# Layer 1's gate and up products of a two-layer encoder by seven block products instead of eight

## The chip, the cores and the metric

One core of one Trainium2 chip. The metric is the device time of one execution in microseconds (us): the time before is the median of three runs, 2474.93 us (2474.85 to 2480.22). Engines are named as in the profile: PE (TensorE, matmuls; PEld is its weight load), DVE (VectorE), ACT (ScalarE), POOL (GpSimd), SP (SyncE, which here only issues DMAs). All times below come from one profiled execution of the kernel before.

## The reference

A trunk of two residual layers on x of shape (1, 1024, 1024) in float32. Layer 0 mixes with a gated MLP and pooled means, layer 1 with RWKV-7 time mixing (a recurrence over chunks of 64 tokens), and each layer is followed by a SwiGLU block; the hidden width is 2816, that is 22 blocks of 128.

```python
D_MODEL = 1024; SEQ = 1024; CHUNK = 64; FFN_HIDDEN = 2816

def swiglu(hn, w_gate, w_up, w_down):
    return (jax.nn.silu(hn @ w_gate) * (hn @ w_up)) @ w_down
...
def wkv7_scan(r, w, k, v, a, b):          # RWKV: one state of 64x64 per head
    def step(state, inp):
        r_t, w_t, k_t, v_t, a_t, b_t = inp
        sa = jnp.einsum('bhvk,bhk->bhv', state, a_t)
        state = (state * w_t[:, :, None, :] + sa[..., None] * b_t[:, :, None, :]
                 + v_t[..., None] * k_t[:, :, None, :])
        return state, jnp.einsum('bhvk,bhk->bhv', state, r_t)
...
# layer: h = h + mixer(rms_norm(h)); h = h + swiglu(rms_norm(h)); at the end rms_norm(h)
```

## The kernel before

The 1024 tokens are two halves of 512, A (h = 0) and B (h = 1). Activations lie with features on the partitions: `H[h]` is 8 tiles of 128x512. Every fp32 product is three matmuls of split operands (`mm3`, L343 to L346): hi·hi, lo·hi and hi·lo, each with a 128x128 weight tile and a 128x512 operand. A gate or up block (128 hidden features, all 1024 inputs) for one half is thus 24 matmuls, and so is a down block for one half. In the names of the profile `ahi`/`alo` are the activations, `whi`/`wlo` and `wdhi`/`wdlo` the weights, `hidhi`/`hidlo` the hidden values.

**Weights.** One list, `plan` (`push`, L103), holds every 128x1024 weight block in order of use. `take` (L131) hands out the next one, starts the loads of the two behind it and splits the next: the load goes to a ring of three `raw` buffers on ACT's DMA queue (L113), the hi part is copied out by ACT (L143), the lo part is subtracted by DVE (L144). Each gate and up block of layer 1 is loaded and split twice, once for each half.

**FFN.** `ffn` (L648) runs groups of blocks: gate and up of each block in the group, `silu(gate)·up` (ACT L662, DVE L670), its split (ACT L673, DVE L674), then the group's down products, which DVE adds to the residual (`h<-h,mm`, L424). In layer 1 and half A, blocks 0 and 1 run beside the projections of the second RWKV half, blocks 2 to 17 in groups of three beside the recurrence, 18 and 19 after it, then `out_proj(1)` and the RMS norm of half B, then 20 and 21 with the final norm of half A. Half B runs all 22 blocks after that.

**Recurrence.** `recur` (L1152) takes 512 tokens in 8 chunks of 64: small matmuls (`sm`, `yp`, L1176) between tiles that ACT, DVE and POOL make. Behind every second chunk stands a step `post`: it takes mean and variance of `yp` (DVE L1353 to L1364, with one operation of POOL, L349), scales it (16 ACT operations, L1370), multiplies and adds on DVE and POOL (L1375, L1376), and transposes the result `ysb` on PE into `sm`. `drive` (L732) interleaves the steps of `ffn` and of `recur` by their costs at `RATIO` 3.0. The instruction scheduler of the language decides the order on each engine from there, with a priority that lets dense work run behind the recurrence's (`AHEAD`, 450); each engine then executes its own list strictly in that order, and only semaphores tie the engines to each other. Within the recurrence, PE's small matmuls keep the order of the program (`ordered`).

**Queues.** Weights and activations `y` come on ACT's queue; SP's queue carries the recurrence's operands, the residual's reload (`reload`, L1472: 2 MB in one DMA) and half of the output.

Of the kernel before, what the change touches and what calls it, by code (L numbers as in the profile page):

```python
# [16 lines left out]
P = 128  # L17
# [15 lines left out]
BESIDE = (4, 2)  # L33
# [3 lines left out]
def tile_trunk(  # L37
# [63 lines left out]
    acts, dests, splits = set(), {}, {}  # L101
# [17 lines left out]
    def split_at(i):  # L119
        if i >= len(plan) or i in ready:  # L120
            return
        load_at(i)
        if i not in raws:
            return
        key, _, view, dest = plan[i]
        raw = raws[i]
        hi, lo = (dest or whl)()
        splits.get(key[0], lambda i, *t: split(*t))(key[1], view(raw), view(hi), view(lo))
        ready[i] = hi, lo
# [131 lines left out]
    n0, n1, a, b = groups_of(BESIDE[0])  # L261
    G0B = n0, n1 + [a], [b]
    n0, n1, a, b = groups_of(BESIDE[1])
    G1A = n0, n1, [a], [b]
# [32 lines left out]
    push_beside(1, push_o(0) + push_f(1, 0, G1A[0]))  # L297
    push_proj(1, ("n1", n_d[1]))
    push_ffn(1, 0, G1A[1])
    push_ffn(1, 0, G1A[2], push_act(("y", 1), y_d[1]))  # L300
    for e in push_o(1):
        e()
    push_ffn(1, 0, G1A[3])
    push_ffn(1, 1)
# [24 lines left out]
    def mmt():  # L329
        return pst("mm")  # L330
# [3 lines left out]

    DENSE = {"mm": ("mm", 5), "aux": ("aux", 3)}
# [15 lines left out]
    def norm_sums(h):  # L351
# [7 lines left out]
        return acc  # L359

# [284 lines left out]
    l0_es.close()  # L645

# [780 lines left out]
    def final_down(h, fs, wd, hid, turned):  # L1427

        with tc.manual_schedule(engines={mybir.EngineType.PE}):
# [14 lines left out]
            products(1, 0)  # L1444
            for j in range(4):
# [119 lines left out]
    def blocks():  # L1565
        yield from out_proj(0, ys, sums_a)
        yield from ffn(1, 0, hnA, f, G1A[0], nd=2, after=spill_a)

# [3 lines left out]
    beside(1, blocks(), [1] * 8 + weights_of(G1A[0]), parts, (8, norm_a))  # L1572
# [10 lines left out]
    hp, hp_es = open_pool(name="ha2", bufs=1, side="left")  # L1583
# [3 lines left out]
    drive(ffn(1, 0, hnA, f, G1A[1]), with_reload(hp, 0, h_d[0, 1], recur(1, wp)), RATIO)  # L1587
# [8 lines left out]
    reload(hb_pool, 1, h_d[1, 1])  # L1596
    ys = open_act(("y", 1), b)
    drive(ffn(1, 0, hnA, f, G1A[2], between=take_act(("y", 1))))
# [4 lines left out]
    for e in (fin_es, hb_es, b_es, hp_es, nxt["a_es"], f_es, ps_es):  # L1603
        e.close()
# [30 lines left out]
```

## Time and profile before

| what | before |
|---|---|
| median of three runs | 2474.93 us (2474.85 to 2480.22) |
| the profiled execution | 2477.63 us; span in the trace 2475.9 us |
| mean granted TensorE clock | 0.989 of full speed |
| second v projection ends, recurrence of half B begins | at about 1613 us |
| recurrence ends (last `post` transposed) | 1881 us |
| `out_proj(1)`, norm of half B | until about 1980 us |
| half B's 22 blocks of layer 1 | about 2000 to 2476 us |

The span is what the trace covers; the execution's own time is 1.7 us longer. A row of the trace's timeline gives start, duration, engine, line, operation, tiles and shapes, and in brackets the idle time before it and what ended it. Matmuls are pipelined: a duration of 0.39 us in a row doesn't mean that the next one starts 0.39 us later; the distance of two starts is the price of one. Windows give, for a stretch, each engine's busy time, the granted clock (1.00 is full speed), the share of the 16 DMA engines' time in use and the GB/s moved.

### The profile page before, as it was taken

What the parts mean: (1) busy time and instruction counts of PE and PEld (TensorE: products, weight loads), DVE (VectorE), ACT (ScalarE), POOL (GpSimd) and SP (SyncE); (2) the same over time, 40 slices, a digit from 0 to 9 for tenths busy, and PEclk for the clock granted to TensorE, in tenths of its full rate; (3) what the DMA queues carried; (4) which work ended last, traced back from release to release, by engine and by line L of the source; (5) the groups of instructions that cost most, each with busy time, mean ns of one, the idle gap of its engine ahead of it and who ended that gap; (6) DMA issues with size and microseconds to landing.
All of it is one profiled execution on the core that took longest, in us unless ns stands there. A gap on an engine that the chain in (4) does not pass through costs nothing.

```text
span 2475.9 us, 37980 instructions
## 1 busy us (share of the span) xinstructions
PE 2406.4 (97%) x15735; PEld 1977.5 (80%) x15735; DVE 1382.7 (56%) x2126; ACT 912.1 (37%) x1369; POOL 244.6 (10%) x262
## 2 busy tenths in 40 slices
PE   8999999999999998999999999989999999999998
PEld 7888888888878787888878777778878778888887
DVE  6445634444875874655548847856555446444443
ACT  6233422222664432432325754433232324322223
POOL 0200000000014400211000133201111000000001
PEclk9999999999999999999999999999999999999999
DMA  5123433323355577542434465695444322433231
GB/s 179 49 60 89 150 102 102 119 86 94 109 176 139 140 208 202 156 127 70 135 112 143 153 168 134 191 234 140 119 128 128 111 85 75 147 102 118 87 98 56
DMA packets 436396, 310.69 MB, mean 125 GB/s; under 512 B 93376, under 2 KB 395584, under 8 KB 435456
## 3 DMA queue, kind: packets, MB, share of 16 engines
q10 hardware_dynamic: 297280, 210.53, 28.6%
q1 hardware_dynamic: 138944, 97.75, 13.8%
q8 instruction: 123, 2.02, 0.3%
q14 instruction: 49, 0.40, 0.1%
HBM read 254.68 MB, written 53.54 MB: 124 GB/s over the span
## 4 chain that ended last, share of the span: by engine, by line
PE 82%; DMA 6%; DVE 5%; ACT 2%; issue 2%; POOL 2%; SPq 0%; ACTq 0%; POOLq 0%; DVEq 0%
PE mm L344 22%; PE mm L345 22%; PE mm L346 22%; PE sm L1176 5%; DMA raw<-y_d 1%; DVE wlo L144 1%; PE yp L1176 1%; DMA raw<-in_ffn_w_down_dram 1%; DMA lnw<-in_rwkv_ln_w_dram 1%; ACT whi L143 1%; PE aux L1097 1%; PE mm L511 1%; PE mm L512 1%; PE mm L513 1%; PE aux L1098 1%
## 5 line engine op out<-in xcount | busy, mean ns | idle before, releaser
L345 PE MATMUL mm<-alo,whi 128*128 128x512 f32 x1952 | 766.7, 393 | 0.9 <-issue 0.8
L346 PE MATMUL mm<-ahi,wlo 128*128 128x512 f32 x1952 | 765.4, 392 | 1.7 <-DVE wlo L144 1.7
L344 PE MATMUL mm<-ahi,whi 128*128 128x512 f32 x1952 | 765.8, 393 | 0.8 <-ACT whi L143 0.8
L143 ACT ACTIVATE whi<-raw 128x1024 fp32r<-128x1024 f32 x288 | 304.6, 1059 | 744.7 <-PE mm L345 605.3
L144 DVE TENSOR_TENSOR wlo<-raw,whi 128x1024 fp32r<-128x1024 f32 x288 | 359.1, 1248 | 289.5 <-ACT whi L143 270.1
L346 PEld LDWEIGHTS mm<-ahi,wlo 128*128 128x128 f32 x1952 | 367.7, 188 | 82.5 <-issue 3.5
L345 PEld LDWEIGHTS mm<-alo,whi 128*128 128x128 f32 x1952 | 367.7, 188 | 79.9 <-issue 2.9
L344 PEld LDWEIGHTS mm<-ahi,whi 128*128 128x128 f32 x1952 | 367.7, 188 | 79.0 <-issue 2.1
L344 PE MATMUL mm<-hidhi,wdhi 128*128 128x512 f32 x624 | 240.5, 395 | 8.1 <-DVE h L424 3.8
L345 PE MATMUL mm<-hidlo,wdhi 128*128 128x512 f32 x624 | 245.0, 393 | 0.4 <-DVE hidlo L674 0.4
L346 PE MATMUL mm<-hidhi,wdlo 128*128 128x512 f32 x624 | 244.9, 392 | 0.0
L424 DVE TENSOR_TENSOR h<-h,mm 128x512 f32<-128x512 f32 x192 | 129.3, 686 | 149.7 <-PE mm L346 148.5
L143 ACT ACTIVATE wdhi<-raw 128x1024 fp32r<-128x1024 f32 x82 | 86.4, 1057 | 249.7 <-DMA raw<-in_ffn_w_down_dram 164.4
L144 DVE TENSOR_TENSOR wdlo<-raw,wdhi 128x1024 fp32r<-128x1024 f32 x82 | 100.2, 1223 | 112.1 <-ACT wdhi L143 112.0
L670 DVE TENSOR_TENSOR sg<-sg,mm 128x512 f32<-128x512 f32 x88 | 60.3, 686 | 157.1 <-PE mm L346 155.3
L344 PEld LDWEIGHTS mm<-hidhi,wdhi 128*128 128x128 f32 x624 | 117.5, 189 | 36.8 <-DVE h L424 6.4
L345 PEld LDWEIGHTS mm<-hidlo,wdhi 128*128 128x128 f32 x624 | 117.8, 189 | 25.7 <-DVE hidlo L674 1.3
L346 PEld LDWEIGHTS mm<-hidhi,wdlo 128*128 128x128 f32 x624 | 117.8, 189 | 24.9
L424 DVE TENSOR_TENSOR hA<-hA,mm 128x512 f32<-128x512 f32 x72 | 48.8, 686 | 77.2 <-PE mm L346 77.0
L349 POOL TENSOR_TENSOR nrs<-nrs,small 128x4 f32<-128x4 f32 x8 | 10.0, 1244 | 667.2 <-DVE nrs L371 667.2
L674 DVE TENSOR_TENSOR hidlo<-sg,hidhi 128x512 fp32r<-128x512 f32 x88 | 65.7, 748 | 10.0 <-ACT hidhi L673 10.0
L344 PE MATMUL mm<-xhi,whi 128*128 128x512 f32 (+1 forms) x160 | 65.3, 408 | 0.0
(299 smaller groups left out, 2886.3 us busy)
## 6 DMA issues: line engine op xcount, KB each, us to landing
raw<-in_ffn_w_gate_dram ACTq DMA_DIRECT2D x88, 512.0 KB
raw<-in_ffn_w_up_dram ACTq DMA_DIRECT2D x88, 512.0 KB
raw<-in_ffn_w_down_dram ACTq DMA_DIRECT2D x88, 512.0 KB
raw<-in_ab_w_in_dram ACTq DMA_DIRECT2D x16, 512.0 KB
raw<-in_ab_w_out_dram ACTq DMA_DIRECT2D x16, 512.0 KB
raw<-in_rwkv_w_r_dram ACTq DMA_DIRECT2D x16, 512.0 KB
raw<-in_rwkv_w_k_dram ACTq DMA_DIRECT2D x16, 512.0 KB
ar_d<-ar SPq DMA_DIRECT2D x16, 512.0 KB
```

What stands on the lines that cost most here:

```text
L143: act.activation(hi, src, AF.Copy)
L144: (eng or dve).tensor_tensor(out=lo, in0=src, in1=hi.bitcast(F32), op=ALU.subtract)
L344: pe.matmul(o, whi, xhi, start=first, stop=False)
L345: pe.matmul(o, whi, xlo, start=False, stop=False)
L346: pe.matmul(o, wlo, xhi, start=False, stop=last)
L424: dve.tensor_tensor(out=H[h][:, m, :], in0=H[h][:, m, :], in1=o, op=ALU.add)
L511: pe.matmul(ops[j], xhi[:, k, sl], whi[:, kk], start=(k == 0), stop=False)
L512: pe.matmul(ops[j], xhi[:, k, sl], wlo[:, kk], start=False, stop=False)
L513: pe.matmul(ops[j], xlo[:, k, sl], whi[:, kk], start=False, stop=(k == KT - 1))
L670: dve.tensor_tensor(out=s, in0=s, in1=o, op=ALU.mult)
L674: dve.tensor_tensor(out=lo, in0=s, in1=hi.bitcast(F32), op=ALU.subtract)
L1176: i = f(*args, **kw)
```

## The change

For two blocks f = 2i and 2i+1 of one matrix, the weights are a 2x2 matrix of quarters (two halves of the 1024 inputs, two blocks), the activations another (two halves of the inputs, two halves A and B of the tokens). The changed kernel forms the four products of blocks and token halves with seven quarter products instead of eight (the Winograd form of Strassen's algorithm): a quarter product is 12 matmuls, and a pair of blocks of one matrix takes 84 instead of 96. Sums of weight quarters (s1 to s4) are made on DVE from the loaded blocks, sums of activations (t1 to t4) once, on DVE, by `combine`. For this, halves A and B must both be there, which half B is only after the recurrence and `out_proj(1)`. So:

- **Ahead** (`ahead_steps`): eight even blocks (0, 2 beside the projections, 4, 6, 8, 10 beside the recurrence, 12, 14 after it) are computed for half A alone, down product included. The first of the seven products, which is the first half of such a block's sum, is copied out to DRAM (`p1_d`). Beside the recurrence thus stand 4 blocks instead of 16; the ratio of `drive` goes from 3.0 to 9.3.
- **Front** (`first_steps`): three even blocks (16, 18, 20) the same way, without down, beside `combine`, which makes t1 to t4 as soon as half B's norm is there.
- **Full** (`full_steps`): for all 11 pairs and both matrices, 22 rounds, the five products that are left (60 matmuls), which give the odd block for half A and both blocks for half B. Round by round the two weight blocks are combined on DVE in the buffers they were loaded into, the psum is read at two points while it goes on accumulating (`now`), the kept product comes back from DRAM, and the hidden values are written to DRAM (`hid_d`).
- **Down** (`down_steps`): the 14 blocks of half A that are left, then the 22 of half B, with hidden values read back from DRAM on SP's queue. The final norm of half A comes with the last group of A's.

Count of instructions in the whole program, before and after: matmuls with 512 columns 9120 and 8856; DVE tensor_tensor of 128x1024 384 and 319, of 128x512 746 and 1098; ACT activations of 128x1024 396 and 331, of 128x512 708 and 852; weight blocks loaded 234 and 212; DMAs on SP's queue 444 and 578. Up to the products beside the projections of layer 1 the order on PE is the same.

```diff
-BESIDE = (4, 2)
+PAIRS = 11
+AHEAD_OF = ([0, 2],), ([4, 6], [8, 10]), ([12, 14],), (16, 18, 20)
...
+    def ahead_steps(groups, hn, fp, nd, nh, after=None, between=iter(())):
...
+            if kind == "gu":
+                b11, b21 = (parts_of(hn, slice(k, k + 4)) for k in (0, 4))
+                w, os_ = [take((k, 1, 0, f)) for k in "gu"], [mmt(), mmt()]
+                for n in range(2):
+                    yield from quarter_steps(os_[n], parts_of(w[n], LO), b11, True)
+                    t = fp.tile([P, HT], F32, tag="p1", bufs=2 if nd else 1, name="p1")
+                    act.activation(t, os_[n], AF.Copy)
+                    sp.dma_start(p1_d[:, f + n, :], t)
+                for n in range(2):
+                    yield from quarter_steps(os_[n], parts_of(w[n], HI), b21, False)
...
+    def full_steps(blocks, kept, x, fp, wp):
+        def weights(i):
+            (a11, a12), (a21, a22) = ((raws[j][:, LO], raws[j][:, HI]) for j in (i - 1, i))
+            s3 = wp.tile([P, HT], F32, tag="s3", bufs=1, name="s3")
+            dve.tensor_tensor(out=s3, in0=a11, in1=a21, op=sub)
+            s1, s2, s4 = a21, a11, a12
+            dve.tensor_tensor(out=s1, in0=a21, in1=a22, op=ALU.add)
+            dve.tensor_tensor(out=s2, in0=s1, in1=a11, op=sub)
+            b = whl()
+            split(s2, *parts_of(b, HI))
+            split(s1, *parts_of(b, LO))
...
+            dve.tensor_tensor(out=s4, in0=a12, in1=s2, op=sub)
...
+        for i, n in blocks:
+            k = i in kept
+            a = mmt()
...
+            b, c, d = take(("full1", i, n))
+            quarter(a, parts_of(b, HI), x["t2"], k)
+            if prev:
+                prev[0]()
+            if k:
+                t1 = tile_("t1")
+                sp.dma_start(t1, p1_d[:, 2 * i + n, :])
+            u2, u3 = tile_("t2"), tile_("t3")
+            now(u2)
+            o = mmt()
+            quarter(o, parts_of(b, LO), x["t1"], True)
+            if prev:
+                prev[1]()
+            quarter(a, d, x["t3"], False)
+            now(u3)
+            dve.tensor_tensor(out=u3, in0=u3, in1=o, op=ALU.add)
+            finish(i, n, 3, u3)
...
+    def down_steps(l, h, groups, wslot, hslot, ahead=True, after=None, between=iter(()), at={}, last=False):
...
-    drive(ffn(1, 0, hnA, f, G1A[1]), with_reload(hp, 0, h_d[0, 1], recur(1, wp)), RATIO)
+    drive(ahead_steps(AHEAD_OF[1], hnA, f, 2, 3), with_reload(hp, 0, h_d[0, 1], recur(1, wp)), 9.3)
...
+    def combine(bc_):
...
+        for k in range(4):
+            b12, b22 = (nt.tile([P, HT], F32, tag="nsq", bufs=2, name="hn") for _ in range(2))
            for m, t in ((k, b12), (k + 4, b22)):
                dve.scalar_tensor_tensor(
                    out=t, in0=H[1][:, m, :], scalar=col(C_FFN + 8 + m), in1=bc_, op0=ALU.mult, op1=ALU.mult
                )
...
            keep(b22, "b22", k)
...
            dve.tensor_tensor(out=t1, in0=b12, in1=b11h, op=sub)
            dve.tensor_tensor(out=t1, in0=t1, in1=b11l, op=sub)
            keep(t1, "t1", k)
...
            dve.tensor_tensor(out=t2, in0=b22, in1=t1, op=sub)
            keep(t2, "t2", k)
...
            dve.tensor_tensor(out=t3, in0=b22, in1=b12, op=sub)
            keep(t3, "t3", k)
...
            dve.tensor_tensor(out=t4, in0=b21h, in1=t2, op=sub)
            dve.tensor_tensor(out=t4, in0=t4, in1=b21l, op=ALU.add)
            keep(t4, "t4", k)
...
+    drive(first_steps(FRONT, hnA, f), combine(norm_bcast(acc[0])), 2.7)
...
+    H[0] = nxt["a"].tile([P, KT, HT], F32, tag="ahi", name="h")
+    sp.dma_start(H[0], hz_d[0])
...
+    exhaust(full_steps(mats(range(PAIRS)), range(PAIRS), x, f, wp))
...
+    prime_b, steps_b = down_steps(1, 1, D1B, wslot, hslot, last=True)
+    prime_a, steps_a = down_steps(
+        1, 0, D1A, lambda f: lw if f == one else wslot(f), lambda f: low[:, 4:6, :] if f == one else hslot(f),
+        at={len(D1A) - 1: prime_b}, last=True,
+    )
+    prime_a(2)
+    reload(hb_pool, 1, hz_d[1])
...
-    exhaust(out_proj(1, ys))
-    hnB = norm_split(1, C_FFN + 8, b)
-    drive(ffn(1, 0, hnA, f, G1A[3], last=True))
-    drive(ffn(1, 1, hnB, f, last=True))
+    drive(steps_a)
+    drive(steps_b)
```

On PE, around the third `post` of the recurrence of half B, before: the eight transposes of `ysb` stand among the dense matmuls of gate and up (`ahi`, `alo`, L344 to L346).

```order
L344 MATMUL mm<-ahi,whi 128x512
L345 MATMUL mm<-alo,whi 128x512
L1176 MATMUL sm<-ident,ysb 128x128 x7
L1176 MATMUL sm<-XT,w_16238 32x32 x16
L346 MATMUL mm<-ahi,wlo 128x512
```

The same place after the change; small matmuls stand at L1498 there and dense ones at L770 to L772, and the first row is the last product of the chunk before the third `post`:

```order
L1498 MATMUL yp<-uv,gt 64x64 x16
L1498 MATMUL sm<-ident,bk 128x128 x8
L1498 MATMUL sm<-XT,gt 32x32 x16
L1498 MATMUL sm<-ident,ysb 128x128 x8
L1498 MATMUL sm<-XT,w_15707 32x32 x16
L1498 MATMUL sm<-uv,gt 64x64 x16
```

The end of the recurrence on PE, after the change, with the fourth `post`:

```order
L1498 MATMUL sm<-Q,XT 64x64 x16
L1498 MATMUL yp<-S,ar 64x64 x16
L1498 MATMUL yp<-uv,gt 64x64 x16
L1498 MATMUL sm<-ident,ysb 128x128 x8
L770 MATMUL mm<-ahi,whi 128x512
L771 MATMUL mm<-alo,whi 128x512
```

No dense matmul stands any more between the last product of `yp` and the transposes of its `post`, for the third and the fourth; for the second there are 5, for the first 44. The 132 dense matmuls that stand behind the first chunk are all placed before the second `post` ends; 156 stand ahead of the first chunk, where some 180 stood.

On DVE, behind `out_proj(1)`, before: the norm of half B (`hn`, L394, and its lo part, L144) among work of blocks 20 and 21.

```order
L371 TENSOR_SCALAR nrs<-aux 128x4
L374 TENSOR_TENSOR ndg<-ident,nrs 128x512
L670 TENSOR_TENSOR sg<-sg,mm 128x512
L144 TENSOR_TENSOR wlo<-raw,whi 128x1024
L674 TENSOR_TENSOR hidlo<-sg,hidhi 128x512
L394 SCALAR_TENSOR_TENSOR hn<-h,vec,aux 128x512 x2
L144 TENSOR_TENSOR alo<-hn,ahi 128x512
```

After, at the same place, the beginning of `combine` (`rt` are its sums, `xlo` and `alo` their lo parts).

```order
L1953 SCALAR_TENSOR_TENSOR hn<-h,vec,aux 128x512 x2
L155 TENSOR_TENSOR wlo<-raw,whi 128x1024
L155 TENSOR_TENSOR hid<-sg,hid 128x512
L1960 TENSOR_TENSOR rt<-hn,ahi 128x512
L155 TENSOR_TENSOR alo<-hn,ahi 128x512
L1961 TENSOR_TENSOR rt<-rt,alo 128x512
L1965 TENSOR_TENSOR rt<-hn,rt 128x512
L1968 TENSOR_TENSOR rt<-hn 128x512
L155 TENSOR_TENSOR wlo<-raw,whi 128x1024
```

From the first `hn` to the last row of `combine` and the first weight sum s2 stand 65 rows on DVE: 8 scalar_tensor_tensor, 3 of 128x1024 and 54 of 128x512. On PE, 144 dense matmuls (Front) stand between the end of `out_proj(1)` and the first product that needs t2.

On SP's queue, where the down blocks begin, after the change: `hid_d_75` and `hid_d_76` are the hidden values of halves A and B, `hd` the buffers they are read back into, `h<-hz_d_79` is the residual of half B.

```order
L733 DMA hid_d_76<-hid 128x1024 x2
L1797 DMA h<-hz_d_79 128x4096
L733 DMA hid_d_75<-hid 128x1024
L733 DMA hid_d_76<-hid 128x1024
L931 DMA hd<-hid_d_75 128x1024 x13
```

The 2 MB of the residual now stand ahead of the first hidden values that are read back. Before, nothing was read back here: the last DMAs of that queue were the residual's reload, behind the recurrence, and the output.

More of the change, by code (lines that the diff above doesn't have):

```diff
@@ L1444, in final_down @@
             products(1, 0)
+            turned = turned or [turn(h, j) for j in range(4)]
             for j in range(4):
@@ L1592, in tile_trunk, with after @@
     hb_pool, hb_es = open_pool(name="hb2", bufs=1, side="left")
-    fin_pool, fin_es = open_pool(name="fin", bufs=1, side="left")
+    reload(hb_pool, 1, h_d[1, 1])
+    ys = open_act(("y", 1), b)
+    drive(ahead_steps(AHEAD_OF[2], hnA, f, 2, 3, lambda m: sp.dma_start(hz_d[0][:, m, :], H[0][:, m, :]), take_act(("y", 1))))
+    acc, add = running_sums(1)
+    def after(m):
+        sp.dma_start(hz_d[1][:, m, :], H[1][:, m, :])
+        add(m)
+    exhaust(out_proj(1, ys, after))
+    for e in (f_es, hp_es):
+        e.close()
@@ L1600, in tile_trunk @@
[L1600 to L1603 removed]
+    drive(steps_a)
+    drive(steps_b)
+    for e in (f_es, fin_es, hb_es, nxt["a_es"], ps_es):
         e.close()
```

305 lines of the change are left out of this document (289 added, 16 removed).

## The prediction

> **What bounds the kernel now.** I read the page's span and engine rows first, then windows by stage over layer 1, then single rows of the timeline.
>
> ```profile
> span 2475.9 us, 37980 instructions
> PE 2406.4 (97%) x15735; PEld 1977.5 (80%) x15735; DVE 1382.7 (56%) x2126; ACT 912.1 (37%) x1369; POOL 244.6 (10%) x262
> ...
> core 0: us, PE busy (x) PEld busy (x) DVE busy (x) ACT busy (x) POOL busy (x), PEclk, DMA share, GB/s
> ...
> 1662.00:1870.00 208.00, 202.75 (x3018) 169.17 (x3017) 118.20 (x250) 63.91 (x126) 30.13 (x26) 0.99 0.44 125
> 1870.00:1970.00 100.00, 98.52 (x436) 80.56 (x435) 47.47 (x59) 32.31 (x49) 5.18 (x3) 1.00 0.45 141
> 1970.00:2030.00 60.00, 56.01 (x233) 45.13 (x232) 26.96 (x35) 13.50 (x16) 0.00 (x0) 0.94 0.27 82
> ...
> 2092.00:2420.00 328.00, 328.00 (x1457) 271.76 (x1456) 143.27 (x170) 94.30 (x127) 7.59 (x8) 1.00 0.35 108
> ```
>
> PE is the bound: 97% of the span, and in half B's stretch (2092 to 2420) it never stops, at the full granted clock. In the recurrence (1662 to 1870) it is idle for only 208 − 202.75 = 5.25 us, because dense matmuls fill each wait of the small ones. So a matmul removed from PE is worth its full interval, and a dense matmul moved out of the recurrence may uncover a wait. The average of 56% for DVE says nothing of single stretches.
>
> The interval, and the way from the end of a product to its reader, are in the timeline:
>
> ```profile
> 2000.17 0.39 PE L344 MATMUL mm<-ahi,whi 128*128 128x512 f32 x1
> ...
> 2000.85 0.39 PE L344 MATMUL mm<-ahi,whi 128*128 128x512 f32 x1
> ...
> 2001.31 0.39 PE L346 MATMUL mm<-ahi,wlo 128*128 128x512 f32 x1
> ...
> 2001.80 0.69 DVE L670 TENSOR_TENSOR sg<-sg,mm 128x512 f32<-128x512 f32 x1 [3.42 <-PE mm L346]
> ```
>
> Three matmuls take 2000.85 − 2000.17 = 0.68 us, so 0.2267 each; the reader starts 0.1 us after the modelled end.
>
> **1. Matmuls removed.** The order counts 9120 − 8856 = 264 fewer: 264 · 0.2267 = **−59.8 us**. All of them come from stretches where PE is full, so I take all of it.
>
> **2. The recurrence.** Of 16 blocks' dense work 4 remain, and the order shows where they run out: between the last `yp` of a chunk and its `ysb` transposes stand 44, 5, 0 and 0 dense matmuls for the four `post` steps. The chain that those transposes wait for is in the timeline of the last `post` of before:
>
> ```profile
> 1863.37 1.15 PE L1176 MATMUL yp<-uv,gt 128*64 128x64 f32 x30
> ...
> 1864.55 2.20 DVE L1353 BATCH_NORM_STATS2 st<-yp 128x6 f32<-128x64 f32 x16 [2.69 <-PE yp L1176]
> 1866.65 1.28 DVE L424 TENSOR_TENSOR h<-h,mm 128x512 f32<-128x512 f32 x2
> ...
> 1868.83 2.91 POOL L349 TENSOR_TENSOR var<-var,small 128x16 f32<-128x16 f32 x1 [34.89 <-DVE var L1362]
> ...
> 1872.05 4.84 ACT L1370 ACTIVATE ysb<-yp,mean,var 128x64 f32<-128x64 f32 x16 [13.48 <-DVE mean L1364]
> ...
> 1876.96 1.29 POOL L1375 TENSOR_TENSOR ysb<-ysb,lnw 128x512 f32<-128x512 f32 x1 [5.22 <-ACT ysb L1370]
> 1878.33 2.15 POOL L1376 TENSOR_TENSOR ysb<-ysb,vch 128x512 f32<-128x512 f32 x1
> ...
> 1881.12 0.27 PE L1176 MATMUL sm<-ident,ysb 128*128 128x128 f32 x1
> ```
>
> From the end of `yp` (1864.52) to the end of POOL's second operation (1880.48) are 15.96 us; two residual additions stand inside (some 1.1 us) that mostly go, and a hand-over comes on top, so 15.0. Before, 73 dense matmuls covered it. After, PE waits behind the transposes, in order: the other small work between `yp` and them is one `ident,bk` and one `XT,gt` group (1.09 + 0.69, rows below). First: 15.0 − 44 · 0.2267 − 1.78 = 3.3. Second: 15.0 − 5 · 0.2267 − 1.78 = 12.1. Third: 13.2. Fourth: 15.0, since nothing stands between and the dense blocks 12, 14 are queued behind it on PE. Sum 43.6.
>
> ```profile
> 1684.73 0.69 PE L1176 MATMUL sm<-XT,w 32*32 32x32 f32 x32
> ...
> 1695.00 1.09 PE L1176 MATMUL sm<-ident,bk 128*128 128x128 f32 x8
> ...
> 1696.02 0.69 PE L1176 MATMUL sm<-XT,gt 32*32 32x32 f32 x32
> ...
> 1696.86 0.38 ACT L1249 ACTIVATE w<-sm 32x256 f32<-32x256 f32 x1
> ...
> 1698.15 0.43 DVE L1250 COPY w<-sm 32x256 f32<-32x256 f32 x1
> ```
>
> Twice (chunks 4 to 5 and 6 to 7) nothing dense stands between `XT,gt` and `XT,w` either. The copy of `w` ends 1.9 us after `XT,gt`, with DVE's queue ahead of it; 1.1 without, twice: 2.2.
>
> A long gap has a second price. The one in the norm of half B shows it:
>
> ```profile
> 1981.07 1.65 PE L344 MATMUL mm<-hidhi,wdhi 128*128 128x512 f32 x3 [3.27 <-ACT hidhi L673]
> ...
> 1982.94 0.63 PE L346 MATMUL mm<-hidhi,wdlo 128*128 128x512 f32 x1
> ...
> 1987.31 0.40 PE L346 MATMUL mm<-hidhi,wdlo 128*128 128x512 f32 x1
> 1987.54 0.39 PE L344 MATMUL mm<-hidhi,wdhi 128*128 128x512 f32 x1
> ```
>
> After 3.27 us of idle time 14 matmuls take 1987.31 − 1981.07 = 6.24 us where 3.17 would do: 3.1 us lost, and the window holds a granted clock of 0.94. The Trainium skill (TensorE: Matmul & The Clock Gate, What's actually happening) puts it at half the clock for a window of some 3.4 us, so 1.7 us lost each time; by that estimate the sum would be some 7 us less, and the row here contradicts it. Three gaps of over 12 us: 9.2.
>
> Against this the 5.25 us that were idle before go. Recurrence: 43.6 + 2.2 + 9.2 − 5.25 = **+50**. Bounds: 30, if the chain is 10 us long with DVE and ACT freed of dense work (4.84 + 1.29 + 2.15 + 2.91 are fixed, 11.2, less their overlap), and 65, if other waits inside a chunk come out too.
>
> **3. Start of the stage.** 26 fewer dense matmuls stand ahead of the first chunk (6 us), mostly hidden: **+2** (−4 to +8).
>
> **4. `out_proj(1)`.** Its transition and the norm cost before 1.48 + 3.99 idle (the two windows 1870 to 2030) and 3.1 at the low clock, 8.6 in all. After, Front's 144 matmuls stand over the norm; 2 to 3 remain, plus what the norm waits for at its start: **−5**.
>
> **5. `combine`.** DVE's prices, by distances of starts:
>
> ```profile
> 1724.99 0.69 DVE L674 TENSOR_TENSOR hidlo<-sg,hidhi 128x512 fp32r<-128x512 f32 x1
> 1725.59 0.68 DVE L1286 TENSOR_TENSOR Q<-akv,sm 128x512 f32<-128x512 f32 x1
> ...
> 1889.01 1.22 DVE L144 TENSOR_TENSOR wdlo<-raw,wdhi 128x1024 fp32r<-128x1024 f32 x1
> 1890.15 1.22 DVE L144 TENSOR_TENSOR wlo<-raw,whi 128x1024 fp32r<-128x1024 f32 x1
> ...
> L394 DVE SCALAR_TENSOR_TENSOR hn<-h,vec,aux 128x512 f32<-128x512 f32 x16 | 11.8, 749 | 2.1 <-PE aux L378 2.0
> ...
> L349 POOL TENSOR_TENSOR nrs<-nrs,small 128x4 f32<-128x4 f32 x8 | 10.0, 1244 | 667.2 <-DVE nrs L371 667.2
> ```
>
> A 128x512 operation costs 0.60, a 128x1024 one 1.14, and a scalar_tensor_tensor 0.66 (0.749 less the 0.09 by which the first row overlaps the second). The 65 rows from the first `hn` to the first s2 take 8 · 0.66 + 3 · 1.14 + 54 · 0.60 = 41.1, with about 1.3 more for pairs where one needs the other: 42.4. They begin when half B's norm is broadcast. The order puts its two matmuls behind 32 and 64 dense ones of Front, 64 · 0.2267 = 14.5 us after `out_proj(1)` ends, and 1.2 for the matmul and hand-over: 15.7. So the first product that needs t2 and s2 can start at 15.7 + 42.4 + 0.8 (ACT's copy) + 0.8 (the lo part) = 60 us after `out_proj(1)`, while Front is through at 144 · 0.2267 + 1.8 = 34.4. PE waits 25.7 and loses 3.1 more by the clock: **+29** (22 with the norm earlier, 34 with Front's own operations late).
>
> **6. Full.** A pair of rounds (gate and up) is 120 matmuls, 27.2 us. DVE has 34 operations of 128x512 in it, 20.4 us, so it is not the bound by count. But PE must wait for the psum to be read before it goes on accumulating: two dense matmuls stand between in the order, 0.45, against 0.1 + 0.69 and a hand-over, some 0.65 us a pair: 11 · 0.65 = 7, and 1.3 for the first round. Before has no such read. The third item is loads:
>
> ```profile
> 1940.15 3.79 DMA raw<-in_ffn_w_up_dram
> ...
> 1888.37 0.63 SPq L1474 DMA_DIRECT2D h<-h_d  x1
> ...
> 1893.20 6.35 ACTq L113 DMA_DIRECT2D raw<-in_ffn_w_up_dram  x1
> ...
> 1901.24 1.06 ACT L143 ACTIVATE whi<-raw 128x1024 fp32r<-128x1024 f32 x1 [9.13 <-DMA raw<-in_ffn_w_up_dram]
> ```
>
> A weight load takes 3.8 us. Since s1, s2, s4 are made in `raw` itself, a buffer comes free only when the round's last weight operation on DVE has read it, and the load for the next round starts then; DVE's row s3 of that round waits about 3.2 us for it, with everything behind it on DVE, the psum reads included. DVE's loop becomes 20.4 + 2 · 3.2 = 27 against PE's 27.9: at the margin. I put +11 on it, 1 us a pair, from between 0 and 37 (the wait in full on PE, half of the rounds). Sum **+19** (8 to 45).
>
> **7. Start of down.** The first group (block 1, 24 matmuls, 5.4 us) is the only cover for hidden values that SP's queue issues behind a 2 MB reload. When the same reload ran before (1888.37), a weight load behind it on another queue was late: ACT waited 9.13 us for it. With 5.4 us covered and a wait of 11: 6 + 3.1 for the clock, **+9** (2 to 14). The Trainium skill (DMA: Bandwidth & Descriptors, Issuing engines are not separate DMA queues) says that all queues share the 16 engines; the rows agree, with the weight late behind SP's transfer.
>
> **8. The rest.** p1 stores and down blocks stand under full PE, and the tail is the same `final_down`: 0 (±5).
>
> **Sum:** −59.8 + 50 + 2 − 5 + 29 + 19 + 9 = +44. Span 2475.9 + 44 = 2520; the execution's own time was 2477.63, which would give 2521.6; that execution lay 2.7 above the median (2474.93), so **2519 us**.
>
> **Rivals.**
> - *Full is bound by DVE and loads.* For it: DVE's loop of 27 us against 27.9 in step 6, and a strict order on DVE, so that one late load delays all behind it. Against: the two products carried over from the round before (`prev`) give PE some slack. With the upper end of step 6 (45 instead of 19) to twice that, 2519 + 26 to 2519 + 71; I take the lower half, about 2556. Chance 0.14.
> - *Not slower: the chain of `post` is not exposed.* If PE found its transposes ready 4.5 us after `yp`, step 2's 43.6 would fall to 9 (0 + 1.6 + 2.7 + 4.5) and the 9.2 at the low clock would go: 44 less, 2475. That is the point from which it decides; with no chain at all, 2468. For it: DVE and ACT carry a quarter of the dense work. Against: ACT's 4.84 and POOL's 2.91 are the chain's own. Chance 0.06.
> - *Only the count decides:* every gap is covered as before, 2475 − 60 = 2415. Against it stand the rows without dense work and DVE's 42 us. Chance 0.04.
> - *The low clock stays through the recurrence.* Idle times as long as the one in step 2 would come again and again:
>
> ```profile
> 1647.76 0.66 PE L1176 MATMUL sm<-ident,bk 128*128 128x128 f32 x4
> ...
> 1657.57 1.11 PE L1176 MATMUL sm<-ident,bk 128*128 128x128 f32 x4 [4.58 <-DVE gt L1223]
> ```
>
> After 4.58 us of idle time four transposes took 1.11 instead of 0.66, 1.7 times. A chunk's small work (1684.73 to 1696.71, less 8 dense matmuls in it) takes 10.2 us at the full clock; six chunks without dense work at 1.55 times, somewhat below the 1.7, would add 6 · 10.2 · 0.55 = 34: 2553. The Trainium skill (TensorE: Matmul & The Clock Gate, HAM oscillation — how this bites in real kernels) describes such a case, where each burst is shorter than the wait behind it. Chance 0.06.
>
> **How the numbers follow.** Forecast 0.70, rivals 0.14, 0.06, 0.04, 0.06. The forecast's own bounds (step 2 −20/+15, step 5 −7/+5, step 6 −11/+26, the others −10/+13) are not all met at once; half of each sum gives 2495 to 2550. The range reaches to the low-clock case and part of full's: **2486 to 2560**, which leaves out some 0.18. About 0.3% (7.4 us) is what a measurement can tell: 2467 to 2482 is "same". Faster: 0.05; same: 0.05; slower: 0.90.
>
> **What would show it.** PE idle ahead of `ysb` transposes (step 2) of 3, 12, 13 and 15 us; one gap of about 26 us before the first full product, with DVE busy throughout (5); in full, waits for `now` reads and for s3 (6); one gap of about 6 at the first `hd` (7). Wrong would be: DVE's 128x512 below 0.6 us, `post` shorter than 11 us, or full's rounds over 14.5 us each.

## The result

| | us |
|---|---|
| before, median of 4 runs | 2477.55 (2474.85 to 2480.22) |
| changed, median of 4 runs | 2517.26 (2513.0 to 2518.88) |
| ratio | 1.0158 (95% interval 1.0138 to 1.0177) |
| changed, profiled execution | 2518.88; span 2517.2, granted clock 0.972 |

The change makes the kernel 1.6% slower. The forecast was 2519 us, within 2486 to 2560. The head of the changed kernel's page, beside that of before in the prediction:

```profile
span 2517.2 us, 38250 instructions
...
PE 2362.1 (94%) x15471; PEld 1936.7 (77%) x15471; DVE 1518.9 (60%) x2413; ACT 935.5 (37%) x1448; POOL 243.2 (10%) x262
...
PE   8999999999999899999999999987689699998998
```

PE is busy 44.3 us less (2406.4 to 2362.1), and yet the span is 41.3 us longer: PE is no longer full. The row of slices (62.9 us each) shows where: 8, 7, 6 and 8 from 1636 us on are the recurrence of half B, and the 6 from 1951 on is where `combine` stands. Windows over these stages (length, busy time and instructions of PE, PEld, DVE, ACT, POOL, then granted clock, DMA share, GB/s):

```profile
1662.00:1745.00 83.00, 81.49 (x1469) 68.54 (x1469) 53.12 (x104) 26.07 (x54) 12.44 (x13) 0.94 0.55 159
1745.00:1855.00 110.00, 64.71 (x1303) 56.31 (x1303) 47.38 (x138) 33.10 (x81) 22.16 (x15) 0.78 0.36 109
1942.00:1985.00 43.00, 18.84 (x71) 14.95 (x71) 40.44 (x66) 19.23 (x31) 0.00 (x0) 0.68 0.40 136
1985.00:2295.00 310.00, 302.74 (x1321) 246.56 (x1319) 230.86 (x366) 103.86 (x171) 0.00 (x0) 1.00 0.48 150
```

The second half of the recurrence (1745 to 1855) has PE busy for 59% of the time at a granted clock of 0.78, where before had 97% over the whole stage. From 1942 to 1985 the roles are turned round: DVE works 40.44 of 43 us, PE 18.84. The full stage (1985 to 2295) runs near PE's limit.

PE's rows with an idle time ahead of them carry nearly all of it; first the recurrence:

```profile
1715.51 0.93 PE L1498 MATMUL sm<-ident,ysb 128*128 128x128 f32 x7
1716.37 0.69 PE L1498 MATMUL sm<-XT,w 32*32 32x32 f32 x32
...
1718.57 0.97 PE L1498 MATMUL sm<-uv,gt 64*64 64x64 f32 x26
...
1756.34 0.45 PE L1498 MATMUL sm<-ident,ysb 128*128 128x128 f32 x1 [9.25 <-DVE ysb L1698]
1759.84 1.76 PE L1498 MATMUL sm<-ident,ysb 128*128 128x128 f32 x7 [3.05 <-POOL ysb L1698]
1761.52 1.06 PE L1498 MATMUL sm<-XT,w 32*32 32x32 f32 x32
1762.52 1.57 PE L1498 MATMUL sm<-uv,gt 64*64 64x64 f32 x26
...
1794.56 0.45 PE L1498 MATMUL sm<-ident,ysb 128*128 128x128 f32 x1 [9.85 <-DVE ysb L1698]
1798.06 1.76 PE L1498 MATMUL sm<-ident,ysb 128*128 128x128 f32 x7 [3.05 <-POOL ysb L1698]
...
1830.44 0.45 PE L1498 MATMUL sm<-ident,ysb 128*128 128x128 f32 x1 [10.54 <-DVE ysb L1698]
1833.93 1.76 PE L1498 MATMUL sm<-ident,ysb 128*128 128x128 f32 x7 [3.05 <-POOL ysb L1698]
```

The first `post` has its 44 dense matmuls and no wait; the other three wait 12.3, 12.9 and 13.6 us, in two parts, for DVE's half of `ysb` and then for POOL's. The rows also show the price of a cold start: after the second `post` seven transposes take 1.76 us where the first's took 0.93, `XT,w` 1.06 for 0.69, `uv,gt` 1.57 for 0.97, which is 1.8 us in all. The Trainium skill (TensorE: Matmul & The Clock Gate, What's actually happening) has half the clock for some 3.4 us, an estimate of 1.7 us lost; these rows agree with it.

Then the stages behind `out_proj(1)`:

```profile
1976.58 0.79 PE L720 MATMUL mm<-xhi,whi 128*128 128x512 f32 x1 [24.16 <-ACT whi L154]
...
1993.67 0.50 PE L720 MATMUL mm<-xhi,s3hi 128*128 128x512 f32 x1 [0.49 <-ACT s3hi L154]
2021.66 0.50 PE L720 MATMUL mm<-xhi,s3hi 128*128 128x512 f32 x1 [0.49 <-ACT s3hi L154]
...
2271.45 0.50 PE L720 MATMUL mm<-xhi,s3hi 128*128 128x512 f32 x1 [1.13 <-DVE t L884]
...
2275.25 0.50 PE L720 MATMUL mm<-xhi,chi 128*128 128x512 f32 x1 [0.78 <-DVE t L884]
...
2302.79 0.77 PE L396 MATMUL mm<-hd,dhi 128*128 128x512 f32 x1 [8.20 <-DMA hd<-hid_d]
...
2389.21 0.80 PE L396 MATMUL mm<-hd,dhi 128*128 128x512 f32 x1 [3.08 <-ACT dhi L154]
```

One wait of 24.16 us for `combine`; in full, ten of 0.49 for `s3hi`, one in each pair of rounds but the last (a pair takes 2021.66 − 1993.67 = 27.99 us for 120 matmuls, 27.2), and in the last pair 1.13 and 0.78 for reads of the psum (L884 is such a read, `now`); 8.20 at the start of down, and 3.08 between the down blocks of A and B, which the prediction had not foreseen.

### The profile page after: what moved, and what is told of

Same layout as the page of the kernel before. It is cut to its first block, busy times and chain, and to the rows that moved or that the text cites. A ratio compares the mean times of both kernels' runs of the same rounds, so it can differ in the third digit from the quotient of the medians.

```text
span 2517.2 us, 38250 instructions
## 1 busy us (share of the span) xinstructions
PE 2362.1 (94%) x15471; PEld 1936.7 (77%) x15471; DVE 1518.9 (60%) x2413; ACT 935.5 (37%) x1448; POOL 243.2 (10%) x262
## 3 DMA queue, kind: packets, MB, share of 16 engines
q8 instruction: 121, 1.98, 0.3%
## 5 line engine op out<-in xcount | busy, mean ns | idle before, releaser
L397 PE MATMUL mm<-alo,whi 128*128 128x512 f32 x1248 | 490.4, 393 | 0.0
L396 PE MATMUL mm<-ahi,whi 128*128 128x512 f32 x1248 | 489.7, 392 | 0.0
L398 PE MATMUL mm<-ahi,wlo 128*128 128x512 f32 x1248 | 489.0, 392 | 0.4 <-DVE wlo L155 0.4
L154 ACT ACTIVATE whi<-raw 128x1024 fp32r<-128x1024 f32 (+1 forms) x267 | 263.6, 988 | 575.8 <-PE mm L397 401.9
L155 DVE TENSOR_TENSOR wlo<-raw,whi 128x1024 fp32r<-128x1024 f32 (+1 forms) x267 | 308.9, 1157 | 213.1 <-ACT whi L154 196.6
L398 PEld LDWEIGHTS mm<-ahi,wlo 128*128 128x128 f32 x1248 | 234.8, 188 | 51.9 <-issue 2.6
L397 PEld LDWEIGHTS mm<-alo,whi 128*128 128x128 f32 x1248 | 234.8, 188 | 50.4 <-issue 2.5
L396 PEld LDWEIGHTS mm<-ahi,whi 128*128 128x128 f32 x1248 | 234.6, 188 | 50.1 <-issue 1.8
L398 PE MATMUL mm<-hidhi,wdlo 128*128 128x512 f32 x368 | 145.7, 396 | 0.0
L396 PE MATMUL mm<-hd,dhi 128*128 128x512 f32 x248 | 98.6, 398 | 11.3 <-DMA hd<-hid_d 8.2
L397 PE MATMUL mm<-hd,dhi 128*128 128x512 f32 x248 | 98.4, 397 | 0.0
L398 PEld LDWEIGHTS mm<-hidhi,wdlo 128*128 128x128 f32 x368 | 70.1, 190 | 14.8
```

Source lines behind the costliest of these rows:

```text
L154: act.activation(hi, src, AF.Copy)
L155: (eng or dve).tensor_tensor(out=lo, in0=src, in1=hi.bitcast(F32), op=ALU.subtract)
L396: pe.matmul(o, whi, xhi, start=first, stop=False)
L397: pe.matmul(o, whi, xlo, start=False, stop=False)
L398: pe.matmul(o, wlo, xhi, start=False, stop=last)
```

## The experiments

Where a row has no other number of runs, the kernel ran once, beside one run of before on the same chip (for the three last but one, the median of seven). The changed kernel's own four runs spread from 2513.0 to 2518.88, so a single time inside that range doesn't differ from it, and such runs are read by their traces.

| run | us | before there |
|---|---|---|
| thin_before | 2531.5 | 2476.86 |
| post_dve | 2513.29 | 2476.86 |
| s3_two | 2537.1 | 2476.86 |
| reload_late | 2516.77 | 2476.86 |
| held4 | 2518.66 | 2479.8 |
| comb_pool5 | 2517.73 | 2479.8 |
| raw4 | 2519.38 | 2479.8 |
| reload_behind | 2515.97 | 2479.8 |
| beside5 | 2510.35 | 2479.17 |
| beside6_fixes, 4 runs | 2495.85 | 2479.17; ratio 1.007 (1.0055 to 1.0085) |
| beside7_fixes, 4 runs | 2494.51 | 2479.17; ratio 1.0061 (1.0044 to 1.0077) |
| no_lo | 2507.93 | 2481.97 |

**thin_before: the recurrence's loss without Strassen.**

```diff
-    G1A = n0, n1, [a], [b]
+    G1A = n0, n1[:1] + [n1[1][:1]], [n1[1][1:]] + n1[2:] + [a], [b]
...
-    drive(ffn(1, 0, hnA, f, G1A[1]), with_reload(hp, 0, h_d[0, 1], recur(1, wp)), RATIO)
+    drive(ffn(1, 0, hnA, f, G1A[1]), with_reload(hp, 0, h_d[0, 1], recur(1, wp)), 9.3)
```

> The kernel before, with the blocks of layer 1 and half A regrouped: only 2, 3, 4 and 5 stand beside the recurrence (288 dense matmuls, as in the changed kernel), the other twelve run after it; no Strassen. Theory (dense matmuls taken from the recurrence uncover the chain of post): about +50 us on before, 2520 to 2540, with 10 to 14 us of idle PE ahead of the ysb transposes of the last three posts. Rival (the recurrence loses little, the cost lies in the new stages): 2475 to 2490.

Measured: 2531.5, that is 54.6 us slower than before. Its timeline of PE shows the same waits as the changed kernel's:

```profile
1756.03 0.45 PE L1176 MATMUL sm<-ident,ysb 128*128 128x128 f32 x1 [9.86 <-DVE ysb L1376]
1759.53 1.75 PE L1176 MATMUL sm<-ident,ysb 128*128 128x128 f32 x7 [3.06 <-POOL ysb L1376]
...
1829.44 0.45 PE L1176 MATMUL sm<-ident,ysb 128*128 128x128 f32 x1 [10.54 <-DVE ysb L1376]
1832.95 1.76 PE L1176 MATMUL sm<-ident,ysb 128*128 128x128 f32 x7 [3.06 <-POOL ysb L1376]
...
1850.25 0.80 PE L344 MATMUL mm<-ahi,whi 128*128 128x512 f32 x1 [9.53 <-ACT whi L143]
```

The last transposes end at 1834.70 us, in before at 1885.60, with 444 fewer dense matmuls ahead of them. Up to that mark the run has thus lost 1834.70 + 444 · 0.2267 − 1885.60 = 49.8 us; in the changed kernel it is 1835.69 + 100.65 − 1885.60 = 50.7, with the same 444. No product here is Strassen's, so the theory holds: taking 12 blocks from beside the recurrence costs some 50 us by itself, most of the 59.8 that 264 matmuls are worth. The rest of the 54.6 came behind the recurrence, where PE waits 9.53 us for its first weights.

**held4: the same four blocks, placed under the posts.** A no-sync edge on PE holds each dense matmul behind the last `yp` of the latest `post` that was emitted before it.

```diff
+    def hold():
+        return tc.issue_after(marks[-1]) if marks else ExitStack()
...
+            with hold():
+                pe.matmul(o, wh[:, k, :], x[0][:, k, :], start=st, stop=False, skip_group_check=True)
...
+            if h and c % 2:
+                marks.append(last[-1])
...
-    drive(ahead_steps(AHEAD_OF[1], hnA, f, 2, 3), with_reload(hp, 0, h_d[0, 1], recur(1, wp)), 9.3)
+    drive(ahead_steps(AHEAD_OF[1], hnA, f, 2, 3), with_reload(hp, 0, h_d[0, 1], recur(1, wp)), 13.0, 4.0)
```

> The changed kernel with the same four blocks beside the recurrence and nothing else moved: on PE, dense matmuls that are emitted behind a post's last yp are held back until it (an order on PE alone), and the first third of them is emitted ahead. In the order 51, 36, 45 and 6 dense matmuls then stand ahead of the transposes of the four posts, where 44, 5, 0 and 0 stood, and nearly none between the small products of a chunk. Theory (it is where the dense matmuls stand, not how many): the waits at the posts fall from 38.8 to some 18 us, the short waits in the chunks grow by some 6 to 10, so 8 to 15 us off: about 2505. Rival (every wait of the recurrence needs its cover, so moving it gains nothing): 2512 to 2520.

Measured: 2518.66, no gain. The waits at the posts did fall; others came in their place, as its PE rows show:

```profile
1654.85 1.10 PE L1505 MATMUL sm<-ar,bk 64*64 64x128 f32 x30 [2.95 <-DVE gt L1552]
...
1723.83 1.10 PE L1505 MATMUL sm<-ar,bk 64*64 64x128 f32 x32 [3.15 <-DMA bk<-bk_d]
...
1768.76 1.48 PE L1505 MATMUL sm<-ar,bk 64*64 64x128 f32 x32 [2.69 <-DMA bk<-bk_d]
...
1827.15 0.45 PE L1505 MATMUL sm<-ident,ysb 128*128 128x128 f32 x1 [11.60 <-DVE ysb L1707]
1830.65 1.75 PE L1505 MATMUL sm<-ident,ysb 128*128 128x128 f32 x7 [3.06 <-POOL ysb L1707]
```

The waits at the posts fell from 38.8 to 19.0 us, as the theory had it, but all other waits of PE between 1640 us and the last transposes grew from 12.6 to 28.1. By the sum used for thin_before, 47.5 us are lost up to the last transposes, against 50.7 in the changed kernel and 44.4 to 50.6 in the six other runs that leave the recurrence alone (s3_two, reload_late, comb_pool5, raw4, reload_behind, no_lo). The rival holds for this placement: the small products wait for `bk` from DRAM and for DVE and ACT inside the chunks too, and the same 288 matmuls of cover buy about the same time there. That no other placement would do better is not shown.

**beside5: one block more.**

```diff
-AHEAD_OF = ([0, 2],), ([4, 6], [8, 10]), ([12, 14],), (16, 18, 20)
+AHEAD_OF = ([0, 2],), ([4, 6], [8, 10], [12]), ([14],), (16, 18, 20)
...
-    drive(ahead_steps(AHEAD_OF[1], hnA, f, 2, 3), with_reload(hp, 0, h_d[0, 1], recur(1, wp)), 9.3)
+    drive(ahead_steps(AHEAD_OF[1], hnA, f, 2, 3), with_reload(hp, 0, h_d[0, 1], recur(1, wp)), 7.5, 0.0)
```

> The changed kernel with block 12 moved from behind the recurrence to beside it: five blocks there instead of four (72 more dense matmuls), one behind it; nothing else moved. Theory (the recurrence has a chain of its own of some 218 us, and PE has room in it for what was taken out): it ends where it did, and 72 x 0.2267 = 16 us go: about 2501. Rival (PE's gaps are where no dense work can be put, as in held4): the recurrence grows by as much, 2512 to 2520.

Measured: 2510.35, under half of the 16 us, and between theory and rival. Up to the last transposes 36.6 us are lost (372 fewer dense matmuls than before stand ahead of them), against 50.7 in the changed kernel and 44.4 to 50.6 in the other runs: the recurrence took in some 8 to 14 of the block's 16.3. But part of that is lost again, since the single block behind it has nothing to stand between its gate and up and its down, and PE waits for its hidden values:

```profile
1856.26 2.50 PE L396 MATMUL mm<-hidhi,wdhi 128*128 128x512 f32 x5 [5.21 <-ACT hidhi L154]
```

**post_dve: POOL out of the chain.**

```diff
-            for q, eng in enumerate((dve, pool)):
+            for q, eng in enumerate((dve, dve if h else pool)):
```

> The changed kernel, with the second half of ysb multiplied and added on DVE instead of POOL in the recurrence of half B. Theory (PE waits in order for the slowest of the chain): the second wait of each uncovered post, 3.05 us for POOL, falls to about 1, so some 6 us off, about 2511. Rival (the wait is for psum or for the transposes before): no change, 2514 to 2519.

Measured: 2513.29, just inside the changed kernel's own range. The rows tell more: the second wait of the three posts went from 3.05 to 1.92 each, 3.4 us in all instead of 6. It did not go to 1, because DVE's second multiply has to wait for ACT, which is still scaling that half (rows of DVE and PE):

```profile
1756.43 0.69 DVE L1697 TENSOR_TENSOR ysb<-ysb,lnw 128x512 f32<-128x512 f32 x1 [0.95 <-ACT ysb L1692]
...
1757.99 1.73 PE L1498 MATMUL sm<-ident,ysb 128*128 128x128 f32 x7 [1.92 <-DVE ysb L1698]
```

**comb_pool5 and no_lo: what sets the start of full.** The first moves the 20 lo parts of `combine` to POOL, the second leaves them out.

```diff
-        def keep(t, to, k):
-            split(t, *(y[:, k, :] for y in x[to]))
+        def keep(t, to, k, eng=None):
+            split(t, *(y[:, k, :] for y in x[to]), eng=eng)
...
-            keep(b22, "b22", k)
+            keep(b22, "b22", k, pool)
...
```

```diff
+        for lo in (x1[1], x2[1]):
+            pool.memset(lo.bitcast(F32), 0.0)
...
-            split(t, *(y[:, k, :] for y in x[to]))
+            act.activation(x[to][0][:, k, :], t, AF.Copy)
```

> The changed kernel with the 20 lo parts of combine subtracted on POOL instead of DVE. Theory (PE's 24.2 us before the first full product are DVE's queue): 19 of these rows stand ahead of the first weight sums, so 19 x 0.60 = 11 us less, gap about 13, run about 2506. Rival (POOL, at 1.26 us each, becomes the end of the chain, or slows DVE): gap 20 to 28, run 2513 to 2522.

> The changed kernel with the 20 lo parts of combine left out: these tiles are set to zero by POOL ahead of combine, so t1 to t4 and b22 are used with their hi parts alone. comb_pool5 moved the same 20 rows and gained nothing. Theory (DVE's queue sets the start of full, and comb_pool5 failed because DVE's other rows grew while POOL worked): 19 rows x 0.60 = 11 us less, PE's 24.2 us wait falls to about 13, run 2503 to 2508. Rival (the wait is for something else, ACT's hi parts or the weights): wait 20 or more, run above 2512.

Measured: with POOL the wait ahead of full is 27.92 us, longer than the 24.16; without the lo parts it is 12.26, and the run 2507.93:

```profile
1965.17 0.80 PE L720 MATMUL mm<-xhi,whi 128*128 128x512 f32 x1 [12.26 <-ACT whi L154]
```

So DVE's queue sets the start of full, at 0.6 us for each row, and the move to POOL failed for another reason. The timelines of POOL and DVE in comb_pool5 show it:

```profile
1955.09 1.71 POOL L155 TENSOR_TENSOR alo<-rt,ahi 128x512 fp32r<-128x512 f32 x1
1956.76 3.39 POOL L155 TENSOR_TENSOR xlo<-rt,xhi 128x512 fp32r<-128x512 f32 x2
...
1955.60 1.75 DVE L1968 TENSOR_TENSOR rt<-hn 128x512 f32<-128x512 f32 x1
1957.27 1.75 DVE L155 TENSOR_TENSOR hid<-sg,hid 128x512 fp32r<-128x512 f32 x1
1958.94 1.39 DVE L1953 SCALAR_TENSOR_TENSOR hn<-h,vec,aux 128x512 f32<-128x512 f32 x2
1960.26 0.68 DVE L1972 TENSOR_TENSOR rt<-ahi,rt 128x512 f32<-128x512 f32 x1
```

While POOL subtracts, most of DVE's 128x512 operations with two operands in SBUF take 1.6 to 1.8 us instead of 0.68. The scalar_tensor_tensor rows, with one operand from PSUM, take 0.73 each beside POOL, about what they take without it (0.749 on average in before).

**s3_two and raw4: the waits in full.**

```diff
-            d = [wp.tile([P, HT], F32R, tag=t, bufs=1, name=t) for t in ("s3hi", "s3lo")]
+            d = [wp.tile([P, HT], F32R, tag=t, bufs=2, name=t) for t in ("s3hi", "s3lo")]
```

```diff
-        raw = wst.tile([P, D], F32, tag="raw", name="raw")
+        raw = wide[0]() if wide and plan[i][0][0] == "full1" else wst.tile([P, D], F32, tag="raw", name="raw")
...
+    wide.append(lambda: wp.tile([P, D], F32, tag="rawx", bufs=1, name="raw"))
```

> The changed kernel with two buffers instead of one for the split of s3 in the full stage. Theory (the eleven waits of 0.49 us per pair come from ACT, which may write s3hi only when PE has read the one before): waits gone, 6 to 9 us off, about 2509, a pair of rounds at 27.2 us instead of 27.99. Rival, as the prediction had it (PE waits for the psum to be read before it accumulates on): no change, 2514 to 2519.

> The changed kernel with a fourth weight buffer in the full stage, for the second block of each round (the s3 split keeps its one buffer). Theory (a load is issued only when the round before has released its buffer, and DVE's s3 waits 2.85 to 3.6 us for it once a pair): that wait goes and the round has room, but PE's own wait for s3hi stays, so 0 to 5 us off, 2511 to 2518. Rival (the order that the scheduler finds matters more than the buffer): some other wait, up to 2530.

Why a buffer: in the changed kernel's timeline ACT writes the next `s3hi` only when PE's last read of the one before is over (PE's two quarters with s3 stand next to each other once a pair).

```profile
2020.55 0.39 PE L721 MATMUL mm<-xlo,s3hi 128*128 128x512 f32 x1
2020.78 0.39 PE L722 MATMUL mm<-xhi,s3lo 128*128 128x512 f32 x1
2020.98 0.63 ACT L154 ACTIVATE s3hi<-s 128x512 fp32r<-128x512 f32 x1 [4.77 <-PE mm L721]
2021.20 0.69 DVE L884 TENSOR_TENSOR t<-t,mm 128x512 f32<-128x512 f32 x1 [1.93 <-PE mm L722]
2021.66 0.50 PE L720 MATMUL mm<-xhi,s3hi 128*128 128x512 f32 x1 [0.49 <-ACT s3hi L154]
```

Measured: s3_two takes 2537.1, 20 us longer instead of 8 shorter. The waits for `s3hi` are gone, as these rows would have it, but the scheduler finds another order with the two buffers, with four waits of PE for reads of the psum (0.33 to 1.49 us) and, nearly every pair, one for the round's weights, which start from a late load (its timeline of DVE and PE):

```profile
2130.57 0.69 DVE L820 TENSOR_TENSOR s<-raw 128x512 f32<-128x512 f32 x1 [3.81 <-DMA raw<-in_ffn_w_up_dram]
...
2104.09 0.50 PE L720 MATMUL mm<-xhi,whi 128*128 128x512 f32 x1 [2.42 <-ACT whi L154]
...
2134.98 0.50 PE L720 MATMUL mm<-xhi,whi 128*128 128x512 f32 x1 [1.77 <-ACT whi L154]
```

A pair takes 2134.98 − 2104.09 = 30.9 us there, 2.9 more than in the changed kernel.

raw4 took 2519.38, with ten waits of 0.49 as they were. It did not do what its theory wanted: DVE's s3 still waits 2.1 to 3.2 us a pair for its load, 2.8 to 3.6 in the changed kernel, so it doesn't show what that wait is worth.

```profile
2035.46 0.69 DVE L821 TENSOR_TENSOR s<-raw 128x512 f32<-128x512 f32 x1 [2.86 <-DMA raw<-in_ffn_w_up_dram]
```

What can be said comes from PE's rows: in the order of the changed kernel no wait of PE in full, behind its first product, ends with these weights, in that of s3_two waits of 0.4 to 2.5 us do. What two s3 buffers would give in the old order was not tried.

**reload_late and reload_behind: the start of down.**

```diff
-                    sp.dma_start(held[f].bitcast(F32), hid_d[h][:, f])
+                    lasthd[:] = [sp.dma_start(held[f].bitcast(F32), hid_d[h][:, f]).ins]
...
-    reload(hb_pool, 1, hz_d[1])
+    with tc.issue_after(lasthd[0]):
+        reload(hb_pool, 1, hz_d[1])
```

> The changed kernel with the 2 MB reload of half B's residual issued one group of down blocks later. Theory (the first hidden values read back are queued behind the reload and share the DMA engines with it): the 8.2 us wait ahead of the second group falls to 0 to 3, 6 to 10 us off, about 2508. Rival (the wait is the way of the last hidden values into DRAM and back): wait stays at 6 to 8, no change.

> The changed kernel with the 2 MB reload of half B's residual put behind the first four reads of hidden values on SP's queue (the run reload_late left the order on that queue as it was). Theory as before: the 8.2 us wait falls to 0 to 4, run about 2510. Rival (the hidden values can only be read when the full stage has released the buffers, and the way takes that long): wait 6 to 8, no change.

reload_late only wrote the reload later in the program, which left its place on SP's queue as it was; it tells nothing (2516.77). reload_behind (the diff) put it behind the first reads:

```profile
2293.00 3.70 SPq L933 DMA_DIRECT2D hd<-hid_d  x3
...
2296.75 0.42 SPq L1799 DMA_DIRECT2D h<-hz_d  x1
...
2299.14 0.66 PE L396 MATMUL mm<-hd,dhi 128*128 128x512 f32 x1 [4.04 <-DVE dlo L155]
```

The wait falls from 8.20 to 4.04, half of it, and is now one for the split weights. So the reload was half of the cause. The time, 2515.97, lies inside the changed kernel's range.

**beside6_fixes and beside7_fixes: the best version found.** Six or seven blocks beside the recurrence, with post_dve, reload_behind and a buffer of its own for the final norm's `u` (the diff is of beside7_fixes, without the lines shown above).

```diff
-AHEAD_OF = ([0, 2],), ([4, 6], [8, 10]), ([12, 14],), (16, 18, 20)
+AHEAD_OF = ([0, 2],), ([4, 6], [8, 10], [12, 14], [16]), ([18],), (20,)
...
-                u = wst.tile([P, D], F32, tag="raw", name="u")[:, :HT]
+                u = fin_pool.tile([P, HT], F32, tag="u", bufs=2, name="u")
...
```

> The changed kernel with six blocks beside the recurrence (4 to 14), one behind it (16) and two in front of full (18, 20), and three small edits: the second half of ysb on DVE, the reload behind the first hidden values, and a buffer of its own for the final norm's u. Theory: 2 x 16.3 = 33 us off in the recurrence, 10.9 - 3.5 = 7 more ahead of full (one block less of cover, but less work on DVE too), 3 + 2 + 3 off by the small edits: about 2486. Rival (the recurrence fills up with the fifth block): 2500 or more.

> The same with seven blocks beside the recurrence (4 to 16), 18 behind it and 20 alone in front of full. Theory: 3 x 16.3 = 49 us off in the recurrence, 15 more ahead of full, 7 off by the small edits: about 2476, as before the change or a little under. Rival (the last posts can take no more): 2485 to 2495, no better than with six.

Measured: 2495.85 and 2494.51, some 10 and 18 us above their theories, some 22 us faster than the changed kernel and still 0.7 and 0.6% slower than before. The seventh block gained next to nothing, as its rival said. With seven blocks the second and third posts have no wait left, but what covers the recurrence is missing ahead of full (PE's rows):

```profile
1849.36 0.45 PE L1500 MATMUL sm<-ident,ysb 128*128 128x128 f32 x1 [10.63 <-DVE ysb L1700]
...
1973.12 0.79 PE L720 MATMUL mm<-xhi,whi 128*128 128x512 f32 x1 [37.37 <-ACT whi L154]
```

37.37 us instead of 24.16 ahead of full; with six blocks 31.19. The 3 us wait between A's and B's down blocks is gone in both, which fits the buffer that `u` no longer takes from the weights; that edit was not tried alone. No version found beats the kernel before: what the seventh block covers in the recurrence it uncovers ahead of full, and the even blocks of half A seem too few for both places.

## Why the prediction was right

By its own steps, in us on the span: the length of each stage less 0.2267 for each dense matmul in it, less the same of before. As in the forecast, the low clock behind the waits of steps 5 and 7 is counted with them.

| step | forecast | measured |
|---|---|---|
| 1 matmuls removed | −59.8 | −59.8 |
| 2, 3 recurrence and its start | +52 | +50.7 |
| 4 `out_proj(1)` and norm | −5 | −1.9 |
| 5 `combine` | +29 | +27.0 |
| 6 full | +19 | +10.6 |
| 7 start of down | +9 | +10.1 |
| 8 the rest | 0 | +4.6 |
| sum | +44 | +41.3 |

The span grew by 41.3. Steps 2 and 3 are the sum shown for thin_before. Full lasts from 1976.58 to 2289.15 (2302.79 less the wait and 24 matmuls), 312.6 for 1320 matmuls, 299.2; of the 13.4 left, 2.8 are the low clock behind `combine`. That the sum comes within 3 us is in part luck: step 6 was 8 too dear, and steps 4 and 8 together 8 too cheap.

- *Step 1* held; the dense interval is unchanged in the rows of full.
- *Step 2* was right in its main term: 38.8 at the posts for the forecast 43.6, and thin_before shows that it is the thinned recurrence. The first post had no wait (forecast 3.3), and the last 13.6 for 15.0. The clock was taken too dear, 3.1 for each gap from a row of dense matmuls; it was 1.8 where small matmuls follow. Waits elsewhere made up for it. From 1600 us to the last transposes they come to 14.8 us, 5.80 of them near 1662, where a down product waits for ACT (its row for `sg` stands there behind a copy of weights); before had 11.7 in all, and the forecast let 5.25 go. held4 shows that such waits grow when the cover is moved to the posts.
- *Step 4* failed in size: 10.0 us were lost there before and 8.1 after. The blocks behind the recurrence start late (waits of 1.98 and 0.72 for their first weights at 1852) and at the low clock, so that little was saved.
- *Step 5* was right in mechanism and size: Front took 34.6 us (forecast 34.4), the first full product came 58.7 us after `out_proj(1)` (forecast 60), the wait was 24.2 (forecast 25.7) and the low clock behind it 2.8 (3.1), and no_lo moved the wait by 11.9 where 19 rows of 0.60 give 11.4.
- *Step 6* was too dear and for the most part wrong in mechanism. It had PE wait for the psum to be read, 0.65 a pair; that wait shows only in the last pair. In the ten others the wait of 0.49 (0.79 a pair with its restart) is for the single `s3hi` buffer. The late load was seen rightly on DVE (forecast 3.2, measured 2.8 to 3.6), but of the 11 us put on it nothing reached PE. That the stage stands at the margin, the first rival, is shown by s3_two: another order costs 20 us.
- *Step 7* had the size (8.2 and 1.9 by the clock, for 6 + 3.1) and half of the mechanism: without the reload ahead of it the wait is 4.04.
- *Step 8*: the wait of 3.08 between A and B, with 3.0 by the clock behind it, was not foreseen; 1.6 went elsewhere, which wasn't looked for.

The rivals: that the chain of `post` isn't exposed, and that the count alone decides, fall with the waits above. (With no chain at all the former's sum is 2519 − 43.6 − 9.2 = 2466, not 2468; nothing hangs on it.) The low clock did not stay: the granted clock was 0.78 over the second half of the recurrence, idle time included, and the small matmuls were at full speed again at 1764, 7.5 us after the wait of the second post had begun to end.

## What to carry to other kernels

Matmuls are worth their interval only where PE is full, and part of them may be there as cover: count what a chain of small steps needs beside it before taking dense work away, and don't count on moving what is left: in the one other placement that was tried, the waits moved with it. An algorithm with fewer products pays for its sums on another engine; where these must all be done before the first product, they are a serial stage, and its price is that engine's rows less what PE can do meanwhile. With a scheduler, a larger buffer is also a new order, so it is tried on the chip and not counted as free.

## What the runs showed of the hardware

POOL's and DVE's subtractions of two operands in SBUF slow each other: DVE's 128x512 operation mostly went from 0.68 to some 1.75 us while POOL was at one, and POOL's from 1.26 (the row of `ysb` in the post, alone) to 1.7. Twenty operations moved to POOL therefore gained nothing. The Trainium skill (GPSIMD Engine Reference, Specifications) states that GpSimd's SBUF interface is shared with VectorE, with contention for DVE instructions that have two SBUF inputs; the trace agrees, with a factor of 2.6 on DVE.

What a wait on PE costs by the clock did not grow with its length. Behind the 12 us of a post, small matmuls lost 1.8 us. Dense matmuls ran 0.43 us apart instead of 0.2267 for a while: they lost 2.8 us behind the wait of 24.16 (14 matmuls from 1976.58 to 1982.55, 5.97 us for 3.17), 1.9 behind that of 8.20, 3.0 behind that of 3.08, and 3.1 behind the 3.27 of before. Behind the waits of 1.98 and 0.72 at 1852 there was no such stretch.
